# An encoder layer on one core: when the first span's result is turned, and when two kinds of PSUM bank are taken

## The chip, the cores and the metric

The kernel runs on one core of one Trainium2 chip. TensorE (PE) multiplies matrices into PSUM, which has eight banks of 128 x 512 fp32 values here; VectorE (DVE), ScalarE (ACT) and GpSimd (POOL) do the rest, and SyncE (SP) issues the DMAs. The metric is the device time of one launch in microseconds (us), and lower is better.

## The reference

One layer over 2048 tokens of width 1024, everything in fp32. After an RMSNorm, one projection gives the inputs of two token mixers: an attention over 64-token chunks (own chunk and eight before, with a relative bias), and an mLSTM, a recurrence over chunks with exponential gates. Both are projected, gated and summed, then projected out and added to the input; a squared-ReLU feed-forward of width 4096 follows. Cut to what the change touches:

```python
logf = jax.nn.log_sigmoid(f_pre)          # gates of the mLSTM
bcum = jnp.cumsum(logf, axis=2)           # their running sums in a chunk
...
x = x + jnp.square(jax.nn.relu(hn @ w_up)) @ w_down
return rms_norm(x, final_norm_g)          # scale of a token: its mean square over 1024 features
```

## The kernel before, in words

**Tiling.** The 2048 tokens are four blocks of 512 (b = 0 to 3). Blocks 0 and 1 are the first half of the work: their input projections run as plain tiles (lines L644 to L646, three matmuls for one fp32 product, each operand split into a high part and a remainder). Most of the rest runs two blocks at a time as a "span" (s = 0 is blocks 0 and 1, s = 1 is blocks 2 and 3), with seven products in place of eight (L727, L755, and in the down projection L644 to L646 again). Operands are split by ScalarE and VectorE: L583 and L585 for weights, L1180 and L1185 for activations.

**The order of the work.** `dense` is the backbone: input projections of blocks 0 and 1, then the output projection and the input projections of span 1, feed-forward up and down of span 0 (`down`), the merge and output projection of span 1 (`project`, with the merge at L1002 and its gates loaded at L994), feed-forward of span 1. Attention (`scores` L1375, L1381, L1390, L1394; `turn` L1406, L1409, L1411; `weigh` L1344, L1354, L1356), the recurrence and the final norm are background threads beside it. The attention of blocks 2 and 3 runs beside the feed-forward of span 0, and spills into the merge.

**The planner.** The program is written by generators that a planner, `Flow`, runs when the kernel is built: a thread yields "wait" for an event, "get" for an item of a pool, or an engine with an estimated time, and then emits its instructions. Pools are the buffers (`temp` has six of 128 x 516 fp32, `ctx` sixteen) and the eight banks. Among blocked threads the one with the lower priority number goes first; the backbone has 5, background 1 to 3. `Order` then sorts each engine's instructions into a list by due time; TensorE keeps the order in which `Flow` emitted them, as far as they are ready. The lists are fixed when the kernel runs. Of the banks, some are kept for the backbone:

```python
elif isinstance(pool, Banks):
    if room - max(0, pool.want - pool.held) < n:
        return False, None
```

`want` is 4 while `down` runs, so background threads share the other four, and 0 in the merge, when everybody takes from all eight.

**The final norm of a span.** `final` goes through the two blocks of a span, h = 0 and h = 1. `final1` squares each feature tile, adds it to a total (L2284, L2287) and multiplies the tile by the norm's gain (L2291). `final_scale` takes a bank, adds up the total over partitions with small matmuls (L2309), and forms the scale r_z on VectorE (L2321) and GpSimd (L2325). `final_out`, eight threads for a block (four token tiles by two halves of the features), turns four 128 x 128 pieces into a bank on TensorE (L2334), multiplies them by r_z on the way out to a buffer (L2345 on ScalarE or L2347 on VectorE) and stores the buffer (L2351). The eight threads of h = 1 start when those of h = 0 have sent theirs.

**The gates.** `gates_far` waits for what a block's gates need, takes a bank and runs `gates_rest`: a logarithm by a series on 128 x 16 values (L1467 to L1489, VectorE but for one exponential), then the running sums by two matmuls into the bank (L1491, L1492), and more small steps that use the same bank up to L1551. It runs once for each block.

Of the kernel before, what the change touches and what calls it, by code (L numbers as in the profile page):

```python
# [44 lines left out]
NS = NB // 2  # L45
# [16 lines left out]
LAST = (3, 1)  # L62
# [150 lines left out]
def act_ns(n, ps=False, ap=0):  # L213
    return (51 if ps else 93) + 0.834 * n + 93 * ap


def dve_ns(n):
    return 70 + 1.042 * n
# [154 lines left out]
class Layer:  # L373
# [1083 lines left out]
                                                  stop=x == len(part) - 1 and k == 3 and j == 1)  # L1457
            fl.spawn(self.gates(b, *bks), 1)

    def gates_rest(self, b, bk):  # L1460
        fl, nc, B, sm = self.fl, self.nc, self.blk[b], self.sm
        V = nc.vector
        v4 = lambda n: sm[n].rearrange("p (a b) -> p a b", a=NT)
        gf = self.gf[b % 2]
        ig, fg = gf[:, :, 0:4], gf[:, :, 4:8]
        yield "dve", 85
        V.scalar_tensor_tensor(v4("a"), fg, -1.0, fg, op0=ALU.mult, op1=ALU.max)  # L1467
        yield "act", 110
        nc.scalar.activation(sm["e"], sm["a"], AF.Exp, scale=-1.0)
        e, d, s, s2, p = (sm[n] for n in ("e", "d", "s", "s2", "p"))  # L1470
        yield "dve", 85
        V.tensor_scalar(d, e, 2.0, None, op0=ALU.add)
        yield "dve", 85
        V.reciprocal(d, d)
        yield "dve", 85
        V.tensor_mul(s, e, d)
        yield "dve", 85
        V.tensor_mul(s2, s, s)
        yield "dve", 85
        V.tensor_scalar(p, s2, 1.0 / 15, None, op0=ALU.mult)  # L1480
        for m in (13, 11, 9, 7, 5, 3):
            yield "dve", 85
            V.scalar_tensor_tensor(p, p, 1.0 / m, s2, op0=ALU.add, op1=ALU.mult)
        yield "dve", 85
        V.scalar_tensor_tensor(p, p, 1.0, s, op0=ALU.add, op1=ALU.mult)
        yield "dve", 85
        V.tensor_scalar(v4("lf"), fg, 0.0, None, op0=ALU.min)
        yield "dve", 85
        V.scalar_tensor_tensor(sm["lf"], p, -2.0, sm["lf"], op0=ALU.mult, op1=ALU.add)  # L1489
        yield "pe", 300  # L1490
        nc.tensor.matmul(bk[:, 0:16], self.tri, sm["lf"], start=True, stop=True)  # L1491
        nc.tensor.matmul(bk[:, 16:32], self.ones[:, 0:1].to_broadcast([P, P]), sm["lf"], start=True, stop=True)  # L1492
        yield "dve", 85
        V.tensor_copy(sm["bc"], bk[:, 0:16])
        yield "dve", 85
        V.tensor_copy(sm["bl"], bk[:, 16:32])
        yield "dve", 85
        V.tensor_sub(v4("u"), ig, v4("bc"))
        yield "pe", 107
        nc.tensor.transpose(bk[:16, 128:256], sm["u"], self.ident)  # L1500
        a, z = self.cum
        yield "dve", 85
        V.tensor_copy(a[:, 64:], bk[:16, 128:256])
        sh = 1
        while sh < P:
            yield "dve", 150
            V.tensor_tensor(z[:, 64:], a[:, 64:], a[:, 64 - sh:192 - sh], op=ALU.max)
            a, z = z, a
            sh *= 2
        yield "pe", 250  # L1510
        nc.tensor.transpose(bk[:, 256:272], a[:, 64:], self.ident[:16, :16])
        nc.tensor.matmul(bk[:, 272:288], a[:, 191:192].to_broadcast([16, P]), self.ident[:16, :16],
                         start=True, stop=True)
        um = v4("um")
        yield "dve", 85
        V.tensor_copy(sm["um"], bk[:, 272:288])
        ms, ml, bl = self.ms, v4("ml"), v4("bl")
        if b > 0:
            yield "dve", 85
            V.tensor_copy(ms[:, 0], ms[:, NT])  # L1520
        for c in range(NT):
            yield "dve", 85
            V.tensor_tensor(ml[:, c], ms[:, c], um[:, c], op=ALU.max)
            yield "dve", 85
            V.tensor_add(ms[:, c + 1], ml[:, c], bl[:, c])
        msf = ms.rearrange("p a b -> p (a b)")[:, :16]
        yield "dve", 85
        V.tensor_tensor(sm["mt"], msf, bk[:, 256:272], op=ALU.max)
        ex = self.ex
        yield "dve", 85  # L1530
        V.scalar_tensor_tensor(ex[:, 0], sm["mt"], -1.0, sm["bc"], op0=ALU.mult, op1=ALU.subtract)
        yield "dve", 85
        V.tensor_sub(ex[:, 1], msf, sm["mt"])
        yield "dve", 85
        V.tensor_sub(ex[:, 2], sm["u"], sm["ml"])
        yield "dve", 85
        V.tensor_sub(ex[:, 3], msf, sm["ml"])
        yield "act", 150
        nc.scalar.activation(ex, ex, AF.Exp)
        yield "dve", 85  # L1540
        V.tensor_scalar(ex[:, 1], ex[:, 1], 0.5, None, op0=ALU.mult)
        yield "dve", 85
        V.tensor_scalar(ex[:, 2], ex[:, 2], C1, None, op0=ALU.mult)
        yield "pe", 428
        for c in range(NT):
            nc.tensor.transpose(bk[:MH, c * P:(c + 1) * P], sm["mt"][:, c * MH:(c + 1) * MH], self.ident)
        yield "act", act_ns(512, True)
        nc.scalar.copy(self.mtt[:MH], bk[:MH])
        yield "dve", dve_ns(512)
        yield "dve", 85  # L1550
        V.tensor_sub(self.mtt[32:32 + MH], bk[:MH], self.mtt[:MH].bitcast(F32))  # L1551
        fl.put(self.banks, bk)
        fl.set(B["gates"])
# [15 lines left out]

    def gates_far(self, b):  # L1570
        yield "wait", [e[0] for e in (self.mix_kept[b - 1][4:] if b > 0 else [])] + [self.blk[b]["gf"]]
        (bk,) = yield "get", self.banks, 1
        yield from self.gates_rest(b, bk)

    def load_rec(self, b, h):
        fl, nc, B = self.fl, self.nc, self.blk[b]
# [750 lines left out]

    def final_out(self, s, h, t, g, scaled, ready, sent):
        fl, nc = self.fl, self.nc
        yield "wait", scaled  # L2330
        (bk,) = yield "get", self.banks, 1
        yield "pe", 107 * 4
        for i in range(4):
            nc.tensor.transpose(bk[:, i * P:(i + 1) * P], self.acc[s][4 * g + i, h][:, t * P:(t + 1) * P],  # L2334
                                self.ident)
        yield "wait", [ready]
        pool = self.temp
        if s == NS - 1 and h == LAST[1]:
            pool = (self.sc, self.wraw)[g]
        (slot,) = yield "get", pool, 1  # L2340
        o = slot[0] if pool is self.sc else slot
        e = yield "act|dve", 650
        r = self.rr[f"z{h}"][:, t:t + 1]
        if e == "act":
            nc.scalar.mul(o[:, :512], bk, r)  # L2345
        else:
            nc.vector.tensor_scalar(o[:, :512], bk, r, None, op0=ALU.mult)  # L2347
        fl.put(self.banks, bk)
        row = (2 * s + h) * T + t * P
        yield "sp", 900, 2000  # L2350
        nc.sync.dma_start(self.io["out"][row:row + P, g * 512:g * 512 + 512], o[:, :512])  # L2351
        fl.put(pool, slot)
        fl.set(sent)
# [138 lines left out]
```

## Time and profile before

| | us |
|---|---|
| median of three runs | 2824.11 |
| lowest, highest run | 2821.86, 2825.01 |
| the profiled execution, time | 2823.55 |
| the profiled execution, first to last instruction (span) | 2821.8 |
| PE busy | 2790.0 |
| DVE busy | 2041.7 |
| ACT busy | 1528.1 |

In all that follows, a time such as 1966.14 is us from the start of the span. A line number such as L2334 is that of the kernel before, with "out<-in" for the tiles that an instruction writes and reads. PEld is TensorE's weight load, which overlaps its matmuls. The granted clock is the share of full speed that TensorE was allowed. "Releaser" means the instruction whose end the waiting one needed, as far as the profile shows.

### The profile page before, as it was taken

To read this page: it belongs to the slowest core of one execution; us is meant where nothing else is said; L and a number is where in the kernel's file an instruction comes from. 1 tells how busy PE (TensorE), PEld (TensorE's weight loads), DVE (VectorE), ACT (ScalarE), POOL (GpSimd) and SP (SyncE) were. 2 spreads that over 40 slices of the span, in tenths; PEclk is the share of its full clock that TensorE was granted. 3 is DMA by queue.
4 is the path that set the end of the run, shared out by engine and by line. 5 is a ranking of instruction groups with operands and counts; after the bars stand their busy time and mean duration, and the time that the engine had idled before them with its cause. 6 is when DMAs were issued, how large, how long until landed. Compare 5 with 4: busy or idle time off the path is not lost.

```text
span 2821.8 us, 39514 instructions
## 1 busy us (share of the span) xinstructions
PE 2790.0 (99%) x13528; PEld 2333.5 (83%) x13528; DVE 2041.7 (72%) x3743; ACT 1528.1 (54%) x2641; POOL 51.3 (2%) x100
## 2 busy tenths in 40 slices
PE   9999999999999999999999999999999999999998
PEld 7887888888878888888888788888788888888887
DVE  7796799668896867886676688789788644456565
ACT  5564577544454545575555566666535655554444
POOL 0010001000000000000000000000000000000000
PEclk9999999999999999999999999999999999999999
DMA  8957748768756667598879776787676656666563
GB/s 275 288 193 254 223 149 300 246 219 297 239 187 215 246 221 266 178 312 308 284 259 302 245 240 205 233 255 257 218 241 240 208 194 201 209 230 210 189 222 134
DMA packets 317737, 662.41 MB, mean 235 GB/s; under 512 B 35552, under 2 KB 62304, under 8 KB 317536
## 3 DMA queue, kind: packets, MB, share of 16 engines
q1 hardware_dynamic: 317536, 659.90, 70.3%
q8 instruction: 106, 1.74, 0.3%
q14 instruction: 95, 0.78, 0.1%
HBM read 462.63 MB, written 197.13 MB: 234 GB/s over the span
## 4 chain that ended last, share of the span: by engine, by line
PE 93%; DMA 3%; DVE 2%; ACT 1%; issue 1%; SPq 0%; POOL 0%; POOLq 0%; DVEq 0%; ACTq 0%
PE bank L727 44%; PE bank L644 12%; PE bank L645 12%; PE bank L646 12%; PE bank L1344 3%; PE bank L1375 2%; PE bank L1406 2%; PE bank L755 2%; DVE wsp L585 1%; PE bank L1667 0%; DMA wsum<-ctx 0%; PE bank L1668 0%; PE bank L1669 0%; DMA wraw<-in_w 0%; PE bank L1653 0%
## 5 line engine op out<-in xcount | busy, mean ns | idle before, releaser
L727 PE MATMUL bank<-r,wsp 128*128 128x512 f32 x5544 | 1263.4, 390 | 1.6 <-ACT r L1182 1.2
L727 PEld LDWEIGHTS bank<-r,wsp 128*128 128x128 f32 x5544 | 1038.7, 188 | 220.8 <-DVE ctx L1834 2.9
L585 DVE TENSOR_TENSOR wsp<-wraw,wsp 128x1024 fp32r<-128x1024 f32 x459 | 560.8, 1222 | 368.4 <-ACT wsp L583 345.7
L583 ACT CAST wsp<-wraw 128x1024 fp32r<-128x1024 f32 x459 | 482.5, 1051 | 497.7 <-PE bank L727 215.3
L644 PE MATMUL bank<-r,wsp 128*128 128x512 f32 x1472 | 591.5, 402 | 4.1 <-ACT r L1180 3.4
L645 PE MATMUL bank<-r,wsp 128*128 128x512 f32 x1472 | 576.8, 392 | 0.2 <-DVE r L1185 0.2
L646 PE MATMUL bank<-r,wsp 128*128 128x512 f32 x1472 | 576.1, 391 | 0.0
L646 PEld LDWEIGHTS bank<-r,wsp 128*128 128x128 f32 x1472 | 277.1, 188 | 59.0
L644 PEld LDWEIGHTS bank<-r,wsp 128*128 128x128 f32 x1472 | 277.7, 189 | 53.6 <-ACT r L1180 3.8
L645 PEld LDWEIGHTS bank<-r,wsp 128*128 128x128 f32 x1472 | 277.9, 189 | 47.6 <-DVE r L1185 0.5
L1834 DVE TENSOR_TENSOR ctx<-bank,ctx 128x512 f32<-128x512 f32 x186 | 126.9, 687 | 102.3 <-PE bank L727 102.1
L1185 DVE TENSOR_TENSOR r<-r 128x512 fp32r<-128x512 f32 x264 | 173.9, 689 | 31.6 <-ACT r L1180 30.8
L1180 ACT CAST r<-r 128x512 fp32r<-128x512 f32 x264 | 158.0, 622 | 61.6 <-DMA r<-u 50.8
L1826 ACT COPY ctx<-bank 128x512 f32<-128x512 f32 x186 | 108.1, 582 | 72.5 <-PE bank L727 68.6
L1390 ACT ACTIVATE sc<-sc,scs 128x640 f32<-128x640 f32 (+4 forms) x128 | 97.7, 765 | 76.1 <-DVE scs L1387 64.4
L2164 ACT ACTIVATE ctx<-ctx 128x512 f32<-128x512 f32 x96 | 60.6, 631 | 101.1 <-DVE ctx L1834 101.1
L1411 DVE TENSOR_TENSOR r<-bank,r 128x512 fp32r<-128x512 f32 (+1 forms) x168 | 96.5, 595 | 21.9 <-ACT r L1409 20.8
L1381 DVE CUSTOM_DVE_ANT_0 sc<-bank,bias 128x320 f32<-128x320 f32 (+3 forms) x240 | 103.0, 461 | 5.7 <-PE bank L1375 4.5
L1344 PEld LDWEIGHTS bank<-r,r 128*128 128x128 f32 x672 | 98.7, 189 | 9.2 <-DVE r L1411 0.4
L1344 PE MATMUL bank<-r,r 128*128 128x256 f32 (+1 forms) x672 | 105.2, 279 | 0.2 <-DVE r L1411 0.2
L1409 ACT CAST r<-bank 128x512 fp32r<-128x512 f32 (+1 forms) x168 | 81.2, 515 | 35.9 <-PE bank L1406 31.9
L602 DVE TENSOR_TENSOR wraw<-wraw,wraw 128x1024 f32<-128x1024 f32 x76 | 92.8, 1222 | 2.0
(247 smaller groups left out, 2766.1 us busy)
## 6 DMA issues: line engine op xcount, KB each, us to landing
wraw<-in_wf SPq DMA_DIRECT2D x178, 512.0 KB, 4.3
wraw<-wsum SPq DMA_DIRECT2D x136, 512.0 KB, 4.1
r<-u SPq DMA_DIRECT2D x224, 256.0 KB, 4.1
wraw<-in_w SPq DMA_DIRECT2D x88, 512.0 KB, 5.0
u<-ctx SPq DMA_DIRECT2D x128, 256.0 KB, 2.6
ctx<-in_wf SPq DMA_DIRECT2D x112, 256.0 KB, 4.4
wsum<-ctx SPq DMA_DIRECT2D x112, 256.0 KB, 4.3
u<-tmp SPq DMA_DIRECT2D x96, 256.0 KB, 3.5
```

The source lines that it names most:

```text
L583: nc.scalar.copy(w[:, 0], raw)
L585: nc.vector.tensor_sub(w[:, 1], raw, w[:, 0].bitcast(F32))
L644: mm(ps, lh, rh, start=first, stop=False)
L645: mm(ps, lh, rl, start=False, stop=False)
L646: mm(ps, ll, rh, start=False, stop=last)
L727: mm(ps, wv[:, x, k, n], a[:, y], start=new and k == 0 and x == y == 0, stop=k == 3 and x == 1, skip_group_check=True)
L1180: self.nc.scalar.copy(dst[:, 0], src)
L1185: self.nc.vector.tensor_sub(dst[:, 1], src, dst[:, 0].bitcast(F32))
L1344: nc.tensor.matmul(bk[:, c0:c0 + w], st, sl[:, x, o:o + w], start=n == 0, stop=n == total - 1)
L1381: nc.vector.tensor_tensor_reduce(out=e[:, x * w:x * w + w], in0=bks[x][:, :w], in1=br[:, j0 + x * w:j0 + x * w + w], op0=ALU.add, op1=ALU. ...
L1826: nc.scalar.copy(t[:, o:o + 512], ps)
L1834: nc.vector.tensor_add(t[:, o:o + 512], ps, t[:, o:o + 512])
```

## The change

It has two parts. In `final_out`, for the first span alone (s = 0), a thread waits for the scale r_z and takes its output buffer before it takes a bank and turns its four pieces; before, it took the bank and turned them first, and then waited for the scale and for a buffer. For the second span the order is as before; the choice of the pool moves up but picks the same one. In `gates_rest`, for all four blocks, the bank is taken behind the steps of the logarithm, just ahead of the first matmul into it; before, `gates_far` took it ahead of them. No instruction is added, removed or resized.

```diff
-    def gates_rest(self, b, bk):
+    def gates_rest(self, b):
...
         V.scalar_tensor_tensor(sm["lf"], p, -2.0, sm["lf"], op0=ALU.mult, op1=ALU.add)
+        (bk,) = yield "get", self.banks, 1
         yield "pe", 300
         nc.tensor.matmul(bk[:, 0:16], self.tri, sm["lf"], start=True, stop=True)
...
     def gates_far(self, b):
         yield "wait", [e[0] for e in (self.mix_kept[b - 1][4:] if b > 0 else [])] + [self.blk[b]["gf"]]
-        (bk,) = yield "get", self.banks, 1
-        yield from self.gates_rest(b, bk)
+        yield from self.gates_rest(b)
...
     def final_out(self, s, h, t, g, scaled, ready, sent):
         fl, nc = self.fl, self.nc
+        pool, slot = self.temp, None
+        if s == NS - 1 and h == LAST[1]:
+            pool = (self.sc, self.wraw)[g]
         yield "wait", scaled
+        if s == 0:
+            yield "wait", [ready]
+            (slot,) = yield "get", pool, 1
         (bk,) = yield "get", self.banks, 1
         yield "pe", 107 * 4
         for i in range(4):
             nc.tensor.transpose(bk[:, i * P:(i + 1) * P], self.acc[s][4 * g + i, h][:, t * P:(t + 1) * P],
                                 self.ident)
         yield "wait", [ready]
-        pool = self.temp
-        if s == NS - 1 and h == LAST[1]:
-            pool = (self.sc, self.wraw)[g]
-        (slot,) = yield "get", pool, 1
+        if slot is None:
+            (slot,) = yield "get", pool, 1
```

## The prediction

> **What bounds the kernel now.** I read the page first, then the waits of TensorE by stretch, then the stretch that the change rewrites, row by row. The page's first and fourth parts:
>
> ```profile
> PE 2790.0 (99%) x13528; PEld 2333.5 (83%) x13528; DVE 2041.7 (72%) x3743; ACT 1528.1 (54%) x2641; POOL 51.3 (2%) x100
> ...
> PE 93%; DMA 3%; DVE 2%; ACT 1%; issue 1%; SPq 0%; POOL 0%; POOLq 0%; DVEq 0%; ACTq 0%
> ```
>
> TensorE is busy 99% of the span and carries 93% of the chain. The change takes no matmul away and adds none, so it can move the time only through what TensorE loses: idle time, and time at a lower clock. The waits of TensorE, asked for the stretch 2010 to 2042 us, where the first span's result is written out, are these (total us, times, longest):
>
> ```profile
> PE bank L1375 <- ACT tmp L2345: 1.7, 2, 1.4
> PE bank L1406 <- DVE sc L1394: 1.4, 1, 1.4
> PE bank L1375 <- DVE tmp L1002: 1.0, 2, 0.5
> PE bank L2334 <- DVE tmp L2347: 0.9, 1, 0.9
> PE bank L1375 <- DVE scs L1381: 0.7, 1, 0.7
> PE bank L644 <- DVE scs L1381: 0.4, 1, 0.4
> PE bank L2334 <- DVE r L1411: 0.3, 1, 0.3
> ```
>
> They add up to 6.4 us in nine waits. L2345 and L2347 are the two evacuations in `final_out`: two waits for one and one for the other, 2.6 us, are matmuls that want a bank in which a turned tile of the result still lies. The other six waits, 3.8 us, belong to attention (L1375 scores, L1406 turns, L1381, L1394 and L1411 beside them) and to the merge L1002.
>
> The same stretch in the view of busy time by window (length, then busy us of PE, PEld, DVE, ACT and POOL with instructions, then the granted clock, the DMA share and GB/s), with the moments after the last waits:
>
> ```profile
> 2010.00:2042.00 32.00, 25.61 (x145) 20.84 (x144) 18.38 (x42) 12.94 (x24) 1.01 (x1) 0.97 0.75 250
> 2036.00:2040.00 4.00, 1.27 (x5) 0.75 (x6) 2.81 (x7) 1.52 (x4) 0.00 (x0) 1.00 0.75 255
> 2040.00:2043.00 3.00, 3.00 (x11) 2.54 (x11) 1.49 (x4) 1.81 (x4) 0.00 (x0) 0.50 1.01 359
> 2043.00:2044.00 1.00, 1.00 (x5) 0.81 (x4) 0.84 (x3) 0.81 (x2) 0.00 (x0) 0.81 0.67 256
> ```
>
> Idle time is 32 - 25.61 = 6.4 us, as in the waits. Behind it the granted clock is 0.50 for three whole microseconds and 0.81 in the fourth: 3 x 0.5 + 0.19 = 1.7 us more are lost. TensorE had worked 1.27 us of the 4 us before.
>
> Where do these waits come from? Timeline rows of PE, DVE, POOL and ACT, from 26 us earlier:
>
> ```profile
> 1966.14 0.60 PE L2334 MATMUL bank<-const,ctx 128*128 128x128 f32 x4
> ...
> 1970.17 1.04 PE L2334 MATMUL bank<-const,ctx 128*128 128x128 f32 x8
> ```
> ```profile
> 1992.16 0.95 PE L2309 MATMUL bank<-ones,wraw 128*128 128x2 f32 x8
> ```
> ```profile
> 1968.58 1.49 DVE L2287 TENSOR_TENSOR wraw<-wraw,tmp 128x512 f32<-128x512 f32 x2
> ```
> ```profile
> 1994.93 1.32 POOL L2325 TENSOR_TENSOR r_z<-r_z,half 128x4 f32<-128x4 f32 x1 [44.81 <-DVE r_z L2321]
> ```
> ```profile
> 1996.28 0.69 ACT L2345 ACTIVATE tmp<-bank,r_z 128x512 f32<-128x512 f32 x1 [1.54 <-POOL r_z L2325]
> ```
>
> Sixteen transposes stand between 1966.14 and 1970.17, four to a tile. So four banks of eight hold finished tiles that nobody may read until the scale r_z exists at 1994.93 + 1.32 = 1996.25. And the scale is itself held up by that: its sum of squares ends at 1968.58 + 1.49 = 1970.07, but the matmuls that add it up over partitions (L2309) need a bank too, and run at 1992.16, when the down projection, for which the other four banks are reserved, hands back its last ones. Attention gets nothing either. Its three matmul lines in three windows each (L1344, then L1375, then L1406; PE and PEld alone):
>
> ```profile
> 1930.00:1966.00 36.00, 4.94 (x32) 4.84 (x32) 1.00 0.63 199
> 1971.00:1992.00 21.00, 0.00 (x0) 0.00 (x0) 1.00 0.57 200
> 1993.00:2068.00 75.00, 7.14 (x48) 7.02 (x48) 0.98 0.70 234
> ```
> ```profile
> 1930.00:1966.00 36.00, 3.00 (x16) 2.61 (x16) 1.00 0.63 199
> 1971.00:1992.00 21.00, 0.00 (x0) 0.00 (x0) 1.00 0.57 200
> 1993.00:2068.00 75.00, 6.61 (x28) 4.46 (x28) 0.98 0.70 234
> ```
> ```profile
> 1930.00:1966.00 36.00, 3.44 (x25) 2.71 (x22) 1.00 0.63 199
> 1971.00:1992.00 21.00, 0.00 (x0) 0.00 (x0) 1.00 0.57 200
> 1993.00:2068.00 75.00, 7.13 (x40) 5.34 (x40) 0.98 0.70 234
> ```
>
> That is 32 + 16 + 25 = 73 attention matmuls in 36 us, then none in 21 us, and 48 + 28 + 40 = 116 left over for the time in which the output projection, the merge and all sixteen result tiles fight for the same banks.
>
> **The change part by part.**
>
> *The scale before the turn.* The four banks are no longer taken at 1966. One of them can go to L2309 soon after 1970 instead of 1992; with the 4.1 us that lie between 1992.16 and 1996.25, the first half's scale is there near 1975 (an estimate from these rows), and its eight tiles can leave before the down projection ends. The second half, which waits for the first to be sent, then starts at once. The sixteen moved transposes cost TensorE what they cost now, and they read nothing of the scale: the new wait lies in the plan, which puts them later in TensorE's list, so no matmul queues behind a stalled one. The eight stores move with them; the DMA share at 1971 to 1992 is 0.57, so they have room. The two waits behind L2345 and the one behind L2347 go, since a tile is evacuated right after it is turned and its buffer is already there: 2.6 us.
>
> *Attention gets the banks.* At 73 / 36 = 2.0 matmuls per us, 21 us hold 43 of the 116. More than a third moves ahead; it comes out of the busy stretch, but most of the rest still runs there. Of the 3.8 us I take half: 1.9 us. The two ends are 0 (no attention moves) and 3.8.
>
> *What the gaps hide.* Two neighbours in the dense stream (timeline):
>
> ```profile
> 1971.28 0.39 PE L645 MATMUL bank<-r,wsp 128*128 128x512 f32 x1
> 1971.51 0.39 PE L646 MATMUL bank<-r,wsp 128*128 128x512 f32 x1
> ```
>
> They start 0.23 us apart and are shown busy for 0.39, so each wait is 0.16 us longer than its gap: nine times 0.16 is 1.4 us, of which (2.6 + 1.9) / 6.4 = 0.7, 1.0 us, goes.
>
> *The clock.* The half rate came behind three waits of 1.4, 0.7 and 1.4 us within 4 us, and the first of them is one for L2345. Without it TensorE would have been busy half of that time and more; I take all 1.7 us, with 0 as the other end. [...]
>
> *The buffer ahead of the bank.* A buffer of `temp` now lies empty while its bank is awaited. Behind it wait the loads of the gates for the merge (L994), which take the same buffers. It holds for the transposes (0.60 for a tile) and the wait for a bank; since half of the tiles leave early, I take 0, with the merge's 1.0 us of waits (L1002), doubled, as the dear end.
>
> *The gate sums' bank.* It is first written here (instructions of the line, first and last start):
>
> ```profile
> L1491 PE MATMUL bank<-g_lf,const x8: 178/220/263, 51.1 to 1777.0; 128*128 128x16 f32 x8
> ```
>
> Four blocks, and the list of TensorE's waits has none on this line. Taking the bank later frees it for about a dozen short VectorE steps each time: 0, but the plan is laid anew from 51 us on (a rival below).
>
> Sum: 2.6 + 1.9 + 1.0 + 1.7 = 7.2 us. The profiled execution took 2823.55 us with a span of 2821.8; the median of the runs shown is 2824.11, 0.56 higher. From the median, 2824.1 - 7.2 = 2816.9.
>
> **The rivals.**
>
> *Attention cannot use the banks* (0.16). It may be held by its own buffers rather than by banks. For it: its 116 last matmuls are spread over 75 us even with banks coming free. Against: the pace was 2.0 per us until the four banks went. Then only the three waits go, with 3 x 0.16: 3.1 us, 2821.0.
>
> *The plan is laid anew* (0.10). Banks are handed out in another order from the first gates on, and a new wait appears far away. The largest inner wait of the whole kernel is
>
> ```profile
> PE bank L644 <- ACT r L1180: 3.4, 1, 3.4
> ```
>
> One more such, with a half-rate spell of 1.7 us, costs 5.1: 2816.9 + 5.1 = 2822.0.
>
> *The half rate stays* (0.06), as remaining waits still bunch: 2816.9 + 1.7 = 2818.6.
>
> *VectorE becomes the bound* (0.16, slower). In the stretch that attention is to fill, VectorE has nearly no room. Windows, then the two largest VectorE steps of attention in the left-over (L1411, then L1381), then the splits of the stretch itself (group of instructions):
>
> ```profile
> 1950.00:1970.00 20.00, 20.00 (x112) 17.14 (x111) 19.43 (x36) 13.69 (x25) 0.12 (x1) 1.00 0.54 175
> 1970.00:1992.00 22.00, 22.00 (x103) 18.30 (x102) 19.80 (x32) 12.98 (x21) 0.00 (x0) 1.00 0.59 208
> ```
> ```profile
> 1993.00:2068.00 75.00, 7.02 (x12) 0.98 0.70 234
> ```
> ```profile
> 1993.00:2068.00 75.00, 6.50 (x28) 0.98 0.70 234
> ```
> ```profile
> L1185 DVE TENSOR_TENSOR r<-r 128x512 fp32r<-128x512 f32 x17 | 10.9, 684 | 0.6 <-ACT r L1180 0.6
> ```
>
> Free are 22 - 19.8 = 2.2 us. A share of 43/116 of these two (13.5 us) is 5.0, doubled for attention's other VectorE steps 10.0; eight evacuations, if all go to VectorE at the 0.69 of the ACT row, are 5.5. That is 10.0 + 5.5 - 2.2 = 13.3 us too much. If the splits that feed the down projection (L1185, L585) are late by all of it and a half-rate spell follows, the time is 2816.9 + 13.3 + 1.7 = 2831.9. It decides from the point where TensorE waits more than 7.2 us for splits. Against it: at 0.23 us each the stretch holds some 91 dense matmuls, which use up about eight operand tiles (`down` takes 16 for 192 matmuls), and VectorE split 17, so nine, 6.2 us, were done ahead of need and can be put off; and from 1950 to 1970 it was busy 19.43 us of 20 with TensorE at 20 of 20.
>
> **How the numbers follow.** About 0.2%, 5.6 us, is what a measurement of this kernel can tell from no change: faster means below 2818.5, slower above 2829.8. The forecast has 0.52 and lies below 2818.5; three rivals with 0.32 lie within; VectorE with 0.16 is slower. The forecast's own bounds: all 6.4 + 1.4 + 1.7 = 9.5 us gone gives 2814.6, and 2812 leaves room for another 2.6 us from waits elsewhere in the kernel. The range goes from 2812 to 2829, which leaves out the slower case and little else.
>
> **What would show it.** Right: L2309's first eight matmuls between 1970 and 1980, every L2334 behind the L2325 of its half, attention's matmuls present where there were none, no wait of PE on L2345 or L2347 in the first span, no clock of 0.50 near 2040. Half right: L2334 late, but L1344, L1375 and L1406 still absent before the down projection ends. Wrong: new waits of L644 to L646 on L1185 or L585, or a wait above 2 us in a stage that the change does not touch.

## The result and the profile after

The changed kernel takes 2812.06 us (median of 6 runs, 2809.85 to 2818.36) against 2824.56 us of the kernel before beside it (6 runs, 2821.86 to 2827.30). The ratio is 0.996, with a 95% interval of 0.9947 to 0.9973: a gain of 12.5 us, between 7.6 and 15 by the interval. Faster was forecast, at 2816.9, a gain of 7.2.

The profiled execution took 2811.24 us, with a span of 2809.5. Its page, first part:

```profile
PE 2785.5 (99%) x13528; PEld 2331.6 (83%) x13528; DVE 2042.4 (73%) x3742; ACT 1528.2 (54%) x2642; POOL 50.3 (2%) x100
```

The work is the same: 13528 matmuls before and after. The merge stretch in the view of busy time by window (length, then busy us of PE, PEld, DVE, ACT and POOL with instructions, the granted clock, DMA share, GB/s), first of the kernel before, then of the changed one:

```profile
1990.00:2070.00 80.00, 73.51 (x391) 61.00 (x390) 55.05 (x114) 36.23 (x62) 2.32 (x2) 0.98 0.71 237
```
```profile
1990.00:2070.00 80.00, 80.00 (x417) 68.04 (x417) 61.52 (x112) 37.26 (x59) 1.01 (x1) 1.00 0.79 262
```

6.5 us of idle time and the lower clock are gone to the last tenth: TensorE has no wait left there. The rows that answer to those of the kernel before, from the timeline of the changed one (PE, then POOL; the turn is now L2340):

```profile
1975.64 0.95 PE L2309 MATMUL bank<-ones,wraw 128*128 128x2 f32 x8
...
1979.63 1.03 PE L2340 MATMUL bank<-const,ctx 128*128 128x128 f32 x8
...
1983.00 0.60 PE L2340 MATMUL bank<-const,ctx 128*128 128x128 f32 x4
```
```profile
1977.40 1.01 POOL L2325 TENSOR_TENSOR r_z<-r_z,half 128x4 f32<-128x4 f32 x1 [14.29 <-DVE r_z L2321]
```

The sum for the scale runs at 1975.64 in place of 1992.16, the scale is there at 1977.40 + 1.01 = 1978.41, and the first turn starts behind it. Attention's three matmul lines (L1344, L1375, L1406; PE and PEld alone) have filled the gap:

```profile
1971.00:1992.00 21.00, 3.91 (x24) 3.39 (x24) 1.00 0.56 183
1993.00:2068.00 75.00, 5.86 (x36) 5.27 (x36) 1.00 0.81 268
```
```profile
1971.00:1992.00 21.00, 2.47 (x12) 1.93 (x12) 1.00 0.56 183
1993.00:2068.00 75.00, 2.96 (x16) 2.34 (x16) 1.00 0.81 268
```
```profile
1971.00:1992.00 21.00, 2.07 (x16) 1.87 (x16) 1.00 0.56 183
1993.00:2068.00 75.00, 4.47 (x30) 3.56 (x30) 1.00 0.81 268
```

24 + 12 + 16 = 52 matmuls where there were none; 36 + 16 + 30 = 82 are left for the merge, where there were 116, so 34 fewer.

The spans differ by 2821.8 - 2809.5 = 12.3 us. By its own rows the merge accounts for about 9.5: 6.4 of waits, 1.7 of half clock and 1.4 that the gaps hide (the prediction's estimate). Another 3.5 lies near 1555 us, where L644 waits for operands that a DMA brings (in the kernel before ScalarE sits idle for 7.04 us ahead of L1180, until `r<-u` lands). Waits of PE first, before and after, then busy time by window:

```profile
PE bank L644 <- ACT r L1180: 3.4, 1, 3.4
```
```profile
PE bank L644 <- ACT r L1180: 1.6, 1, 1.6
```
```profile
1540.00:1570.00 30.00, 26.42 (x119) 21.36 (x118) 16.36 (x32) 11.30 (x24) 1.32 (x1) 0.94 1.02 341
```
```profile
1540.00:1570.00 30.00, 27.99 (x133) 22.36 (x132) 17.31 (x33) 11.54 (x24) 1.31 (x1) 1.00 1.03 355
```

The wait is 1.8 shorter, and the half clock that came behind it in the kernel before (3.4 us of it, 1.7 lost) is missing in the changed one. That part is not the change's, as the last experiment shows.

The start times of matmuls allow a second account. From the last L727 ahead of the down projection to the first one behind the merge it is 583.4 us in the kernel before (1528.5 to 2111.9) and 569.5 in the changed one (1530.0 to 2099.5). Less what each loses near 1555, 5.1 and 1.6, the gain between is 10.4, so the rows leave about 1 us of it unnamed. The rest of the kernel is 1.6 us longer in the changed profile.

### The profile page after: what moved, and what is told of

The parts are those of the page before. It is cut to its first block, busy times and chain, and to the rows that moved or that the text cites. A ratio compares the mean times of both kernels' runs of the same rounds, so it can differ in the third digit from the quotient of the medians.

```text
span 2809.5 us, 39519 instructions
## 1 busy us (share of the span) xinstructions
PE 2785.5 (99%) x13528; PEld 2331.6 (83%) x13528; DVE 2042.4 (73%) x3742; ACT 1528.2 (54%) x2642; POOL 50.3 (2%) x100
## 4 chain that ended last, share of the span: by engine, by line
PE 95%; DMA 2%; DVE 2%; ACT 1%; issue 1%; SPq 0%; POOLq 0%; DVEq 0%; ACTq 0%
PE bank L727 44%; PE bank L644 12%; PE bank L645 12%; PE bank L646 12%; PE bank L1344 3%; PE bank L1375 2%; PE bank L1406 2%; PE bank L755 2%; DVE wsp L585 0%; PE bank L1667 0%; PE bank L1668 0%; PE bank L2340 0%; PE bank L1669 0%; PE bank L1653 0%; DMA r<-mfar 0%
## 5 line engine op out<-in xcount | busy, mean ns | idle before, releaser
L727 PE MATMUL bank<-r,wsp 128*128 128x512 f32 x5544 | 1263.6, 390 | 1.6 <-ACT r L1182 1.1
L727 PEld LDWEIGHTS bank<-r,wsp 128*128 128x128 f32 x5544 | 1038.6, 188 | 221.1 <-DVE ctx L1834 3.1
L585 DVE TENSOR_TENSOR wsp<-wraw,wsp 128x1024 fp32r<-128x1024 f32 x459 | 561.1, 1223 | 375.3 <-ACT wsp L583 357.6
L644 PE MATMUL bank<-r,wsp 128*128 128x512 f32 x1472 | 590.0, 401 | 1.6 <-ACT r L1180 1.6
L644 PEld LDWEIGHTS bank<-r,wsp 128*128 128x128 f32 x1472 | 277.0, 188 | 50.0 <-ACT r L1180 2.4
L1185 DVE TENSOR_TENSOR r<-r 128x512 fp32r<-128x512 f32 x264 | 174.2, 690 | 30.4 <-ACT r L1180 29.1
L1180 ACT CAST r<-r 128x512 fp32r<-128x512 f32 x264 | 157.7, 621 | 56.3 <-DMA r<-u 49.4
L1381 DVE CUSTOM_DVE_ANT_0 sc<-bank,bias 128x320 f32<-128x320 f32 (+3 forms) x240 | 103.3, 462 | 6.2 <-PE bank L1375 4.9
L1344 PE MATMUL bank<-r,r 128*128 128x256 f32 (+1 forms) x672 | 105.9, 279 | 0.2 <-DVE r L1411 0.2
L1344 PEld LDWEIGHTS bank<-r,r 128*128 128x128 f32 x672 | 98.3, 189 | 9.2 <-DVE r L1411 0.5
```

What stands on the lines that cost most here:

```text
L585: nc.vector.tensor_sub(w[:, 1], raw, w[:, 0].bitcast(F32))
L644: mm(ps, lh, rh, start=first, stop=False)
L727: mm(ps, wv[:, x, k, n], a[:, y], start=new and k == 0 and x == y == 0, stop=k == 3 and x == 1, skip_group_check=True)
L1180: self.nc.scalar.copy(dst[:, 0], src)
L1185: self.nc.vector.tensor_sub(dst[:, 1], src, dst[:, 0].bitcast(F32))
L1344: nc.tensor.matmul(bk[:, c0:c0 + w], st, sl[:, x, o:o + w], start=n == 0, stop=n == total - 1)
```

## The experiments

Each was compared with the kernel before on the same chip. The diffs show their main lines. "Waits" are those of TensorE between 1990 and 2070 us in one profile.

| kernel | median us | before us | ratio, 95% interval | waits, us |
|---|---|---|---|---|
| the change | 2812.06 | 2824.56 | 0.9960, 0.9947 to 0.9973 | 0 |
| e1, the result's part alone | 2813.03 | 2823.47 | 0.9958, 0.9945 to 0.9970 | 0 |
| e2, the gate sums' part (blocks 0 to 2) | 2823.05 | 2823.47 | 1.0000, 0.9992 to 1.0009 | 6.4 |
| e3, scale first | 2813.32 | 2823.47 | 0.9964, 0.9951 to 0.9976 | 1.6 |
| e4, buffer first | 2819.44 | 2823.47 | 0.9985, 0.9976 to 0.9994 | 3.3 |
| e5, late scale | 2818.61 | 2823.89 | 0.9980, 0.9971 to 0.9990 | 0 |
| e6, three banks held | 2815.21 | 2823.89 | 0.9965, 0.9956 to 0.9975 | 0 |
| e7, second span too | 2813.43 | 2823.89 | 0.9955, 0.9937 to 0.9974 | 0 |
| e8, two tiles turned at a time | 2813.83 | 2823.89 | 0.9961, 0.9948 to 0.9975 | 0 |
| e9, banks held and late scale | 2813.11 | 2825.06 | 0.9953, 0.9935 to 0.9971 | 0 |
| e11, turned after the down projection | 2817.20 | 2825.06 | 0.9971, 0.9959 to 0.9983 | 1.8 |

### Which part of the change, and which step of it

**e1: the result's part alone.** `gates_far` and `gates_rest` as before.

```diff
-    def gates_rest(self, b):
+    def gates_rest(self, b, bk):
...
-        (bk,) = yield "get", self.banks, 1
         yield "pe", 300
...
-        yield from self.gates_rest(b)
+        (bk,) = yield "get", self.banks, 1
+        yield from self.gates_rest(b, bk)
```

> The change in final_out alone; the gate sums' bank is taken where it was before. Bank theory (the four banks held from 1966 to 1996 us starved attention and the scale): all of the gain is here, 2810 to 2815 us, no wait of TensorE on L2345 or L2347 in the first span and no spell of half clock near 2040. Rival, that the plan laid anew from the first gates on carries a part: 2816 to 2822.

Measured: 2813.03 us, 10.4 below the kernel before, and no wait of TensorE from 1960 to 2070. The whole gain is in `final_out`.

**e2: the gate sums' part alone**, for blocks 0 to 2. Block 3's late bank alone was not tried.

```diff
+        if bk is None:
+            (bk,) = yield "get", self.banks, 1
         yield "pe", 300
...
-        (bk,) = yield "get", self.banks, 1
+        bk = None
+        if not (b < 3):
+            (bk,) = yield "get", self.banks, 1
         yield from self.gates_rest(b, bk)
```

> The gate sums' bank taken behind the logarithm for blocks 0 to 2 (block 3 as before), and final_out as before. Bank theory: no gain, 2822 to 2827, with the same waits of TensorE between 2010 and 2042 us and the same half clock behind them. Rival, plan laid anew: 2 to 5 us away from the kernel before, either way, with a wait gained or lost between 0 and 1600 us.

Measured: 2823.05 us, a ratio of 1.0000. The merge is the old one, for TensorE to a hundredth:

```profile
1990.00:2070.00 80.00, 73.52 (x391) 61.01 (x390) 55.08 (x113) 36.15 (x61) 2.32 (x2) 0.98 0.71 236
```

So this part is worth nothing that can be measured, and the plan laid anew from 51 us on brings nothing by itself.

**e3: the scale first, the buffer behind the turn**, and **e4: the buffer first, no wait for the scale.** Both with the gates as before; against e1:

```diff
         if s == 0:
             yield "wait", [ready]
-            (slot,) = yield "get", pool, 1
```
```diff
         if s == 0:
-            yield "wait", [ready]
             (slot,) = yield "get", pool, 1
```

> final_out of the first span waits for the scale before it takes a bank, but takes its buffer behind the turn as before; gates as before. Bank theory: the scale is what held the banks for 26 us, so most of the gain is here, 2811 to 2816. Buffer theory (a tile in a bank waits for a buffer, and this is what stops TensorE): waits on L2345 and L2347 stay, 2818 to 2823.

> final_out of the first span takes its buffer ahead of the bank, but turns without waiting for the scale; gates as before. Bank theory: tiles still lie turned in banks until the scale is there, attention still has none from 1971 to 1992, so little or no gain, 2821 to 2829. Buffer theory: the three waits behind L2345 and L2347 go, 2816 to 2821.

Measured: 2813.32 us for e3, 2819.44 for e4. The scale carries nearly everything, as the bank theory said. But e4 gained 4.0 us where that theory gave it nothing. Its waits of PE (total us, times, longest):

```profile
PE bank L644 <- DVE r L1411: 1.5, 1, 1.5
PE bank L644 <- DVE scs L1381: 0.9, 1, 0.9
PE bank L1344 <- DVE r L1411: 0.3, 1, 0.3
PE bank L2309 <- DVE tmp L1002: 0.3, 1, 0.3
PE bank L644 <- DVE tmp L1002: 0.3, 1, 0.3
```

None is for an evacuation of the result, and the half clock is gone with them (1.00 from 1990 to 2070). Attention was as starved as before (no matmul of its lines from 1971 to 1992, 116 behind 1993). So a good part of the merge's waits went without attention moving at all. The prediction's account of those waits did not cover that.

### Moved attention, early tiles, or banks that are not locked

Three things change at once: attention runs under the down projection; half of the result's tiles leave before the merge; and in the merge no turned tile lies in a bank while it waits for a scale or a buffer. The next four kernels put them back one by one.

**e5: attention moved, tiles late.** The changed kernel; the first scale waits for the down projection's end.

```diff
         yield "wait", summed[:1] if s > 0 else summed
+        if s == 0:
+            yield "wait", [self.down_end[0]]
```

> The changed kernel, but the first half's scale of the first span waits for the end of the down projection, as it came in the kernel before; the banks stay free for attention, while all sixteen result tiles leave during the merge. Attention theory (the gain is attention's work moved under the down projection): most of the gain stays, 2811 to 2816. Drain theory (the gain is that eight result tiles leave before the merge and no longer fight there for banks and buffers): it is lost, 2819 to 2825, with waits of TensorE between 2000 and 2045 us.

Measured: 2818.61 us, a gain of 5.3 of the 12. There is no wait before 2070, against the drain theory, but there are new ones in the output projection, where neither kernel had any (waits of PE from 2090 to 2200):

```profile
PE bank L727 <- DVE ctx L2049: 1.0, 1, 1.0
PE bank L727 <- ACT wsp L583: 1.0, 1, 1.0
PE bank L727 <- ACT r L1183: 0.8, 1, 0.8
PE bank L727 <- DVE r L1188: 0.7, 2, 0.4
```

That projection begins at 2099.7 of a span of 2815.6, in the changed kernel at 2099.5 of 2809.5. With late tiles nothing is lost in the merge and some 6 us behind it, of which these waits are 3.5. The last two loads of `yp` are issued at 2108.9 and 2113.8, 9 and 14 us behind the projection's first matmul, in place of 2093.4 and 2097.6, ahead of it. That late tiles keep `ctx` buffers from these operands is not shown, and e9 below speaks against it.

**e6: attention starved, tiles early.** The changed kernel, with three background banks held empty.

```diff
+            if s == 0 and h == 0:
+                fl.spawn(self.hold(scaled[0]), -1)
...
+    def hold(self, scaled):
+        yield "wait", scaled[4:5]
+        got = yield "get", self.banks, 1
+        got += yield "get", self.banks, 1
+        got += yield "get", self.banks, 1
+        yield "wait", [self.down_end[0]]
+        self.fl.put(self.banks, *got)
```

> The changed kernel with three of the four background banks held empty from the scaling of the first half's tiles to the end of the down projection; the scale and the result tiles can go through the one that is left. Attention theory: attention starves as before and the gain is lost, 2819 to 2826. Drain theory: the tiles leave early through one bank and the gain stays, 2811 to 2816.

Measured: 2815.21 us, and no wait in the merge. Attention was starved more than asked for (26 matmuls from 1930 to 1966, where the changed kernel has 74), and left far more to the merge (L1345, L1376 and L1407 here; PE and PEld alone):

```profile
1993.00:2068.00 75.00, 12.51 (x72) 10.72 (x72) 1.00 0.78 255
```
```profile
1993.00:2068.00 75.00, 7.86 (x40) 6.36 (x40) 1.00 0.78 255
```
```profile
1993.00:2068.00 75.00, 9.36 (x60) 6.99 (x60) 1.00 0.78 255
```

72 + 40 + 60 = 172 attention matmuls, against 116 before the change, and TensorE still never stops. The attention theory, which the prediction shared in part, falls: moving attention isn't needed.

**e9: both put back.** e5 and e6 together; what is left of the change is the order of scale, buffer and bank.

> The changed kernel with both obstacles of the kernel before put back: three background banks held empty to the end of the down projection, so attention starves, and the first half's scale waits for that end, so all sixteen tiles leave during the merge. What is left of the change is only that no turned tile lies in a bank while it waits for its scale or its buffer. If that alone stops the waits of the merge: none above 1 us in sum between 2000 and 2070, 2814 to 2820 (the later waits near 2120 us may come, as in the run with the late scale). If moved attention or early tiles are needed too: 3 to 7 us of waits there, 2819 to 2826.

Measured: 2813.11 us, the full gain. The merge by windows, then attention's three lines:

```profile
1990.00:2070.00 80.00, 80.00 (x467) 69.69 (x466) 63.24 (x147) 41.27 (x78) 1.50 (x4) 1.00 0.79 257
```
```profile
1993.00:2068.00 75.00, 11.17 (x72) 10.38 (x72) 1.00 0.79 255
```
```profile
1993.00:2068.00 75.00, 6.24 (x32) 4.97 (x32) 1.00 0.79 255
```
```profile
1993.00:2068.00 75.00, 8.91 (x60) 7.10 (x60) 1.00 0.79 255
```

164 attention matmuls in the merge; the first sum for the scale at 1987.14, nearly as late as before; half of the tiles turned by 2014 (1997 before) and the last at 2059. Yet TensorE is busy 80.00 of 80. That no turned tile lies in a bank while it waits is enough by itself. The later waits of e5 do not come back, though the tiles leave later still (the last evacuation starts at 2063.5, in e5 at 2050.4), and its last two loads of `yp` are issued at 2101.7 and 2107.9, around the projection's first matmul at 2105.1; why they come there and not here stays open.

**e11: attention moved, banks locked in the merge.** The kernel before, where a tile is turned only after the down projection's end, and then holds its bank until its scale and its buffer are there.

```diff
         yield "wait", scaled
+        if s == 0:
+            yield "wait", [self.down_end[0]]
         (bk,) = yield "get", self.banks, 1
```

> The kernel before, where the first span's tiles are turned only after the down projection's end: attention has its banks from 1971 to 1992, but in the merge each turned tile holds its bank until its scale and its buffer are there, as before. If tiles in banks are what stops TensorE in the merge: waits of 2 us or more stay between 1995 and 2070, 2816 to 2823. If moved attention suffices: no such waits, 2812 to 2817.

Measured: 2817.20 us, a gain of 7.9. Its waits of PE:

```profile
PE bank L644 <- DVE tmp L2350: 1.0, 1, 1.0
PE bank L2337 <- ACT tmp L2348: 0.6, 1, 0.6
PE bank L2337 <- DVE tmp L1357: 0.2, 1, 0.2
```

1.8 us are left of 6.4. Two of the three are waits for an evacuation of the result (L2348 and L2350 here), and none is of an attention matmul, of which 63 are left behind 1993. Banks were locked in the merge all the same, though not for the first half's scale, which is there before any tile is turned (POOL):

```profile
1979.45 1.33 POOL L2326 TENSOR_TENSOR r_z<-r_z,half 128x4 f32<-128x4 f32 x1 [28.78 <-DVE r_z L2322]
```

The last of the sixteen tiles' transposes starts at 2026.7 and the last evacuation at 2053.7 (2023.6 and 2043.1 in the kernel before). e3 is a second case, which the table shows with 1.6 us of waits: its last transpose starts at 2018.5, its last evacuation at 2042.5, and 60 attention matmuls are left behind 1993. So each suffices for most of the waits: with banks never locked attention may do its work in the merge (e9), and with attention gone ahead locked banks cost little (e11, e3). The kernel before had both at once. In the change both go, so which of the two took a given wait away cannot be said.

### How many banks, and more of the same

**e8: at most two tiles turned at a time**, in the kernel before.

```diff
         yield "wait", scaled
+        if s == 0:
+            yield "get", self.turned, 1
         (bk,) = yield "get", self.banks, 1
```

> The kernel before, where at most two tiles of the first span's result lie turned in banks at a time. If the block was that the scale could not get a bank (it waits on banks held by tiles that wait for the scale), two free banks undo it, the scale comes near 1975 us and all of the gain is there: 2811 to 2816. If attention needs all four banks: half of the gain, 2816 to 2821. If the buffer ahead of the bank matters most: 2820 to 2825.

Measured: 2813.83 us, and no wait in the merge. The first sum for the scale runs at 1975.5, as in the changed kernel. Two locked banks of eight cost nothing. This confirms the circle that the prediction described: tiles wait in banks for a scale, and the scale waits for a bank.

**e7: the same order for the first half of the second span too.**

```diff
-        if s == 0:
+        if s == 0 or h != LAST[1]:
             yield "wait", [ready]
```

> The changed kernel with the same order of scale, buffer, bank for the first half of the second span's result too. Beside it runs no attention, and TensorE has no wait there, so all theories expect no change against the changed kernel: 2809 to 2817. Slower by 1 to 3 us if the tiles, turned later, push out the last half's.

Measured: 2813.43 us, as the changed kernel within the intervals. None of the kernels beats it clearly.

**Both kernels profiled again**, unchanged.

> The kernel before, profiled a second time. If the wait of L644 on the operand from u near 1555 us (3.4 us in its first profile, 1.6 in the changed kernel's) is an accident of one execution, it comes out anywhere between 1.0 and 4.3, the spread over the kernels run here; the waits between 2010 and 2042 us come out as 6.4 us again, within 0.5. If it belongs to the plan: 3.4 again, within 0.3.

> The changed kernel, profiled a second time. Accident of one execution: its wait near 1555 us lies anywhere between 1.0 and 4.3. Belonging to the plan: 1.6 again, within 0.3. Between 1990 and 2070 us TensorE has no wait again, either way.

Second profiles: 2821.85 us with a wait of 1.7 near 1555, and 2817.48 us with 1.9. First ones: 3.4 and 1.6. Over all kernels run here it lies between 1.0 and 4.3 (e1), whatever the plan, so it is an accident of the execution. The merge repeats: 6.0 us of waits in the kernel before, none in the changed one. But the half clock in the merge was twice as long this time in the kernel before (windows):

```profile
2030.00:2045.00 15.00, 11.89 (x52) 9.45 (x51) 9.34 (x20) 6.58 (x13) 0.00 (x0) 0.77 0.79 283
```

15 x 0.23 = 3.4 us are lost there in place of 1.7. The second pair still lies only 4.4 us apart, mainly since the changed kernel had three spells of half clock that its first profile did not have:

```profile
224.00:240.00 16.00, 13.69 (x78) 11.88 (x77) 5.76 (x16) 6.16 (x22) 0.00 (x0) 0.89 0.51 180
720.00:736.00 16.00, 13.80 (x53) 10.61 (x52) 11.94 (x17) 5.78 (x8) 0.00 (x0) 0.89 0.82 271
984.00:1000.00 16.00, 13.92 (x55) 11.05 (x54) 11.16 (x15) 5.07 (x8) 0.00 (x0) 0.89 0.97 372
```

Each costs 16 x 0.11 = 1.8 us, some 5 together. A fourth one, near 1564 (0.59 from 1564 to 1568), is matched by one near 1558 in the kernel before (0.69 from 1556 to 1560). From the last L727 ahead of the down projection to the first one behind the merge it is now 582.2 us in the kernel before (1527.9 to 2110.1) and 569.9 in the changed one (1535.9 to 2105.8); less the losses near 1555, 3.4 and 3.6, the gain between is 12.5, where the first pair had 10.4. What the merge is worth is therefore better read from its own stretch, 10 to 13 us by these two pairs, than from two spans.

## Why the prediction was right, and where it wasn't

- **What bounds the kernel, and where it loses time**: held. Nothing but the merge stretch changed beyond chance.
- **The circle of scale and banks**: held. The sum ran at 1975.64 where 1970 to 1980 was named; the scale came at 1978.41 for an estimate of 1975.
- **The waits for the evacuations**, 2.6 us: all gone, as forecast.
- **"Attention gets the banks", half of 3.8 us**: the step that was mis-sized, and its reason was incomplete. All 3.8 went. The amount that ran early was about right (52 matmuls for 43, though only 34 fewer were left for the merge), but the waits did not need it: with 164 left in the merge (e9) they are gone too. It took late attention and locked banks together to make most of them; the releasers L1002 and L1381 named only who freed a bank last among the few that still went round. Taking the rows' releasers for causes split 6.4 us into two parts that were one.
- **What the gaps hide**, 1.0 of 1.4: followed the same step; all 1.4 went.
- **The clock**, 1.7 us: gone as forecast, with 1.00 throughout the merge. The second profile of the kernel before lost 3.4 there, so the term was the smaller of the two sizes seen.
- **Sum**: with the full 3.8 and 1.4 it is 9.5 us and 2814.6, the lower bound given for the forecast. The median came 2.5 us below that, within the interval. By the matmuls' start times the stretch is worth 10.4 and 12.5 in the two pairs of profiles, so some of the excess is the stretch's own; in the first pair 3.5 more was luck near 1555, and 1.6 was lost elsewhere.
- **The buffer ahead of the bank**, 0: held, with the scale ahead of both; e1 lies at e3 within the intervals, and the merge's waits on L1002, 1.0 before, are none (1.6 in e3, where the buffer comes last). Without the scale it is worth 4.0 (e4), which the prediction had no term for.
- **The gate sums' bank**, 0: held (e2).
- **The rivals**: VectorE was indeed nearly full in the stretch, but TensorE did not stop (changed kernel, windows):

```profile
1970.00:1992.00 22.00, 22.00 (x143) 19.58 (x142) 21.11 (x49) 14.40 (x28) 1.01 (x1) 1.00 0.57 188
```

  The splits done ahead of need were put off, as the argument against that rival had it: from 1971 to 1992 there are 12 of L1185 in place of 17, and 2 of L585 in place of 4. "Attention cannot use the banks" fell with 52 matmuls, "the plan is laid anew" with e2, "the half rate stays" with a clock of 1.00.

## What to carry to other kernels

A bank, or any scarce buffer, should be taken last, when all else that its holder waits for is there; a holder that waits for something which itself needs such a bank closes a circle, and the trace shows it as finished tiles beside a stretch in which a background stage has no instruction at all. When several waits in one stretch name different releasers, ask first whether one shortage lies behind them all, and size them together. Where two causes must coincide to stop an engine, undoing either one shows nearly the whole gain, so neither experiment alone proves its cause.

## What the runs showed of the hardware

The half rate of TensorE came after less idleness than the prediction reckoned with, and not every time. That TensorE keeps its full rate when it is busy half of the time and more was the prediction's estimate. In the second profile of the kernel before, the half rate followed one gap of 1.7 us, with TensorE busy 1.78 us of 3.41, just over half (windows; PE busy first, the clock third from the end):

```profile
1554.10:1557.51 3.41, 1.78 (x7) 1.18 (x7) 2.03 (x3) 2.57 (x4) 0.00 (x0) 1.00 1.05 399
1557.51:1560.92 3.41, 3.41 (x12) 2.70 (x11) 2.48 (x5) 0.76 (x2) 0.00 (x0) 0.50 1.04 410
```

3.41 x 0.5 = 1.7 us are lost, as much as behind the merge's bunch of waits in the first profile. In the changed kernel a gap of 1.6 us at the same place left the clock alone, with TensorE busy 1.80 us of 3.41:

```profile
1554.40:1557.81 3.41, 1.80 (x8) 1.12 (x6) 0.62 (x2) 0.86 (x2) 0.00 (x0) 1.00 1.05 398
1557.81:1561.22 3.41, 3.19 (x15) 2.10 (x14) 3.15 (x5) 2.46 (x4) 0.00 (x0) 1.00 1.05 404
```

The merge's bunch of waits in the kernel before left TensorE busy 1.24 us of 3.41, and the clock is then 0.50 for as long:

```profile
2036.56:2039.97 3.41, 1.24 (x5) 0.72 (x6) 2.26 (x7) 0.96 (x3) 0.00 (x0) 1.00 0.70 229
2039.97:2043.38 3.41, 3.41 (x12) 2.90 (x13) 1.74 (x5) 2.19 (x5) 0.00 (x0) 0.50 1.01 362
```

Near 985 the changed kernel has a gap of 2.0 us in its first profile and of 2.1 in its second. The second is followed by half clock, the 0.89 from 984 to 1000 above. The first is not, though TensorE was busy only 1.42 us of the 3.41 up to its end:

```profile
981.97:985.38 3.41, 1.42 (x7) 0.86 (x6) 3.26 (x5) 1.04 (x1) 0.00 (x0) 1.00 1.04 410
985.38:988.79 3.41, 3.41 (x15) 2.82 (x16) 3.38 (x5) 0.00 (x0) 0.00 (x0) 1.00 1.04 407
```

A gap of 1.7 us was thus followed by the half rate and one of 2.0 us was not, so the length of a single gap does not decide it, and neither does the busy time just ahead, as these profiles show it. What does decide it is not shown here.
